# Hybrid decoder layer on one core: gate product moved ahead of the gated unit, S5 taps in 64-row tiles, another order of the last weight units, and TensorE in the last layer norm

## The chip, the cores and the metric

One Trainium2 chip, one of its cores, one launch. The metric is device time in microseconds. All data are float32; TensorE takes most operands as fp32r, split into a high and a low part.

## The reference

One decoder layer for 256 positions of width 1024:

```
proj = x @ W_in -> q, k, v, z_a (512 each), u, z_s (512 each), g_a, g_s (1024 each)
A    = (attention(q, k, v, bias) * silu(z_a)) @ W_attn_proj       8 heads x 64, causal
y    = Re(C h) + D u,  h_t = Abar h_(t-1) + Bbar u_t              32 groups x 16 channels x 64 states
B    = (GLU(gelu(y) @ W_glu) * silu(z_s)) @ W_ssm_proj
mix  = (sigmoid(g_a) * A + sigmoid(g_s) * B) @ W_out
ple  = sigmoid(x @ W_ple_gate) * (p @ W_ple_proj)
out  = LayerNorm(alpha * x + mix + ple) * g + b
```

The bias is a table of 32 buckets by 8 heads, looked up by the distance of two positions.

## The kernel before

**Weights in units.** Every large weight is cut into units of 256 rows by 512 columns (512 KB), 70 of them, in the list `units`: 40 of `w_in`, 4 of `w_ap`, 4 of `w_glu`, 8 of `w_pg`, 2 of `w_pp`, 4 of `w_sp` (units 58 to 61) and 8 of `w_out` (62 to 69). `load_next` issues the DMA of the next unit from SP's queue into one of five `raw` buffers (line 117). `split_next` makes the parts: ScalarE copies `raw` to `whi`, rounded (line 144), VectorE subtracts to get `wlo` (line 145). `whi` and `wlo` have three buffers each, so the split of a unit waits until TensorE is done with the unit three before. A unit is then 24 matmuls of 256 columns (`t_chunk`) or 12 of 512 (`n_chunk`): high by high, high by low, low by high, all from line 149. The last four units don't use `whi` and `wlo` but tiles that are free by then (`tail_w`): high parts in the buffers `xh` and `xl`, which held the split input and are read last by the `w_pg` matmuls, low parts in `tb` and `sc` of the attention.

**Order.** TensorE's order is written out by hand: it runs the matmuls in the order of the code. For the other engines a planner orders the instructions ahead of the run; what stands in `tc.high_priority()` goes first. The loop over `steps` (one step per unit up to `w_sp`) puts the next load, the evacuation of the chunk just finished and the split of unit i + 2 at high priority, then the unit's matmuls, then what `order` lists for that step. `AT` gives the steps of the work in between: `bt` the transposes of the S5 input matrix (`s5_btT`, line 383, copied out of PSUM by ScalarE on line 385), `x` the S5 inputs (`s5_xm`, `s5_x`, then the scan and `s5_h`), `sc` the attention scores and the softmax that follows one step later (`a_scores`, `a_exp`, exponentials on line 587, scaling on line 592), `kb` and `cb` the S5 kernels, `tr` and `out` the attention's transposes and products, `y` the S5 outputs. The small products use four PSUM banks (`aux`), the chunks four others (`acc`).

**S5 output.** Four positions make a step of the scan. Within such a step the input acts through taps: `s5_kbd` spreads the 16 x 16 blocks of each tap over 128 x 128 block-diagonal matrices (`Kbd`), and `s5_yt(t)` runs four matmuls with them on `uT`, of 256, 192, 128 and 64 columns. `s5_y(t)` adds the part of the carried state: 32 matmuls of 128 rows by 32 columns, into four strips of 32 output partitions. A float32 matmul (not fp32r) shows as two matmul instructions in the trace. `s5_bounce` brings the input through DRAM into `U`, where a partition holds a channel and a lag.

**End.** After step 61, `w_out`: units 62 to 65 hold its first 512 rows and 66 to 69 the rest. Each serves row tile 0 and row tile 1 (128 positions each, parameter `s` of `wo_mm`). The operands are the merged branches, `mh0`, `ml0` for the first 512 rows and `mh1`, `ml1` for the rest, written by `ev_ys` (lines 801 to 806) after units 59 and 61. `ln_in` adds the product to `xb` and takes statistics; `ln_out` normalises, on VectorE in pieces and on ScalarE and POOL for the rest, and stores. `ev_pp` (lines 788, 790) adds the per-layer term to `xb` after units 56 and 57.

Of the kernel before, what the change touches and what calls it, by code (L numbers as in the profile page):

```python
# [18 lines left out]
P = 128  # L19
# [3 lines left out]
H = 8  # L23
# [9 lines left out]
AT = dict(bt=24, x=27, sc=23, kb=27, cb=29, tr=31, out=32, y=35)  # L33
# [12 lines left out]
C_ID, C_MK, C_J, C_OH = 0, P, P + 8, P + 8 + NPH  # L46
C_W = C_OH + 257
# [10 lines left out]
def hybrid_layer_kernel(ctx: ExitStack, tc, xT, x, pT, w_in, w_ap, w_sp, w_out, par, bp, cp,  # L58
# [33 lines left out]
    mask = cs[:, C_MK:C_MK + 8]  # L92
    jmul = cs[:, C_J:C_J + NPH]
    onehot = cs[0:32, C_OH:C_OH + 257]
# [13 lines left out]

    def load_next(pieces=1):
        i = st["load"]  # L110
        if i >= len(units):
            return
        st["load"] += 1
# [8 lines left out]
    def split_next(pieces=1):  # L122
        i = st["split"]
        if i >= len(units):
            return
        st["split"] += 1
# [5 lines left out]
        else:  # L132
            if j == 0:
# [69 lines left out]
    def par_loads():  # L203
        nc.sync.dma_start(cs, cst)
        nc.sync.dma_start(br, bp)
        nc.sync.dma_start(cr, cp)
    dk = T([P, 4], "dk")
    rb = T([32, 8], "rb")
# [212 lines left out]
    def s5_kbd():  # L421
        p_ = st5["kp"]
        kb = st5["Kbd"] = T([P, 4, 4, P], "Kbd")
        V.tensor_tensor(out=kb.rearrange("p t u (g c) -> p (t u) g c", c=16),
                        in0=bc(p_[:, 0:256].rearrange("p (tu c) -> p tu c", c=16), 2, 8),
                        in1=bc(bc(mask, 1, 16), 3, 16), op=ALU.mult)
        for t in range(4):
            V.scalar_tensor_tensor(kb[:, t, 0, :], ident, dk[:, t:t + 1], kb[:, t, 0, :],
                                   op0=ALU.mult, op1=ALU.add)
# [86 lines left out]
    def s5_yt(t):  # L516
        p_ = st5[f"yp{t}"] = aux()
        kb = st5["Kbd"]
        for tau in range(4):
            n = (4 - tau) * NJ  # L520
            mm(p_[:, tau * NJ:4 * NJ], kb[:, t, tau, :],
               uT[:, t, 0:4 - tau, :].rearrange("p l j -> p (l j)"), tau == 0, False)

    def s5_y(t):
# [7 lines left out]
        if t == 0:  # L532
            st5["y"] = T([P, 4, S], "U")
# [14 lines left out]
    def a_bias():  # L548
        p_ = aux()
        nc.sync.dma_start(rb, relb)  # L550
        mm(p_[0:8, 0:257], rb, onehot, True, True)
        r8 = T([8, 384], "pt", bufs=2)
        V.memset(r8[:, 0:127], NEG)
        A.activation(r8[:, 127:384], p_[0:8, 0:257], AF.Copy)
        rs = dr.tile([8, 384], F32, name="scr_r")
        nc.sync.dma_start(rs, r8)
        nc.sync.dma_start(tb, bass.AP(tensor=rs.tensor, offset=rs.offset,
                                        ap=[[1, P], [384, H], [1, 256]]))
# [196 lines left out]
    def ev_glu(n):  # L755
# [19 lines left out]
        return f  # L775
    for n in range(2):
        t_chunk(4, lambda: (yh[0], yl[0]), ev_glu(n))

    n_chunk(8, xop, ev_tanh(new("tg0", "CAb0", (P, 2, 512))))
# [45 lines left out]


    order = {}

# [28 lines left out]
    at(AT["kb"] + 1, lambda: s5_kbm(1), s5_kbd)  # L857
# [4 lines left out]
    for t in range(4):  # L862
        at(AT["y"] + 2 * t, lambda t=t: s5_yt(t))
        at(AT["y"] + 1 + 2 * t, lambda t=t: s5_y(t))
    at(44, load_x)

    pend = None
    for i, (f, ev) in enumerate(steps):
        with tc.high_priority():
# [4 lines left out]
            split_next(2 if i < 2 else 1)  # L874
# [137 lines left out]
```

## Time and profile before

| | us |
|---|---|
| median of 3 runs | 242.12 (242.01 to 242.9) |
| the profiled execution | 242.09 |
| its span | 240.3 |
| TensorE busy | 230.3 |
| VectorE busy | 188.2 |
| ScalarE busy | 140.2 |
| POOL busy | 15.9 |
| loaded and stored through DRAM | 42.47 MB read, 1.59 MB written |

Engines: PE is TensorE's matmuls, PEld its weight loads (beside the matmuls), DVE VectorE, ACT ScalarE, POOL GpSimd, SP the queue that issues DMAs. A busy share is an average over stages with different limits, and a busy TensorE is not one at its peak, since matmuls overlap: what a stage costs is read from the times at which its instructions start. A row of the trace in order of time has the start, the time that the merged instructions took, engine, line, operation, output and inputs, shape and count, and in brackets the idle time of the engine just before, with what ended it. All times count from the start of the span.

### The profile page before, as it was taken

The numbers are of one execution on the slowest core, as the hardware profiler recorded it, in microseconds if no ns is written. First come the engines' busy times: TensorE is split into PE (matmuls) and PEld (weight loads), VectorE is DVE, ScalarE is ACT, GpSimd is POOL, SyncE is SP. The second block draws the span as 40 slices with busy tenths as digits, with TensorE's granted clock in tenths as the row PEclk, the third lists the DMA queues.
The fourth block names the chain that finished last, engine by engine and source line by source line (L and its number), as shares of the span: only waits on it lengthen the run. The fifth ranks groups of instructions, "written<-read, shape, count | busy, mean of one in ns | idle before, by whom it ended". The sixth has DMA issues, their size and how long they took to land.

```text
span 240.3 us, 5066 instructions
## 1 busy us (share of the span) xinstructions
PE 230.3 (96%) x2042; PEld 212.6 (88%) x2042; DVE 188.2 (78%) x333; ACT 140.2 (58%) x222; POOL 15.9 (7%) x17
## 2 busy tenths in 40 slices
PE   8899999999999999999999999999999999999970
PEld 6899999999978899998998999999888889988760
DVE  2879999999899986878999744485674479997395
ACT  4847554845588389999734955335565353775021
POOL 4000000000000005000000000072000000000031
PEclk9999999999999999999999999999999999999998
DMA  5999998977634484323743663664555655660013
GB/s 162 331 343 357 354 238 242 353 232 215 196 93 118 147 255 119 110 92 97 232 150 136 207 213 110 197 245 162 189 174 191 199 202 170 186 190 0 3 44 131
DMA packets 26374, 44.37 MB, mean 185 GB/s; under 512 B 4200, under 2 KB 7280, under 8 KB 26352
## 3 DMA queue, kind: packets, MB, share of 16 engines
q1 hardware_dynamic: 26064, 43.75, 57.5%
q8 instruction: 16, 0.26, 0.4%
q10 hardware_dynamic: 288, 0.31, 0.4%
q14 instruction: 6, 0.05, 0.1%
HBM read 42.47 MB, written 1.59 MB: 183 GB/s over the span
## 4 chain that ended last, share of the span: by engine, by line
PE 77%; ACT 10%; DMA 5%; DVE 4%; SPq 2%; issue 1%; ACTq 0%
PE acc L149 68%; PE aux L149 8%; DMA raw<-in_w_in 5%; ACT whi L144 4%; ACT sc L587 2%; ACT sc L592 2%; ACT CAb L436 1%; DVE wlo L145 1%; SPq L191 1%; SPq L189 1%; DVE xb L930 1%; DVE xb L920 1%; DVE st L910 1%; DVE xb L908 1%; PE aux L598 0%
## 5 line engine op out<-in xcount | busy, mean ns | idle before, releaser
L144 ACT ACTIVATE whi<-raw 128x1024 fp32r<-128x1024 f32 (+2 forms) x71 | 70.7, 997 | 59.9 <-PE acc L149 52.9
L145 DVE TENSOR_TENSOR wlo<-raw,whi 128x1024 fp32r<-128x1024 f32 (+2 forms) x71 | 81.9, 1154 | 30.3 <-ACT whi L144 29.9
L149 PE MATMUL acc<-xh,whi 128*128 128x256 f32 x288 | 47.7, 287 | 0.8 <-ACT whi L144 0.8
L149 PE MATMUL acc<-xl,whi 128*128 128x256 f32 x288 | 45.8, 281 | 0.0
L149 PE MATMUL acc<-xh,wlo 128*128 128x256 f32 x288 | 45.6, 280 | 0.0
L149 PEld LDWEIGHTS acc<-xh,whi 128*128 128x128 f32 x288 | 39.3, 190 | 2.3 <-ACT whi L144 1.3
L149 PEld LDWEIGHTS acc<-xl,whi 128*128 128x128 f32 x288 | 39.3, 189 | 0.0
L149 PEld LDWEIGHTS acc<-xh,wlo 128*128 128x128 f32 x288 | 38.9, 188 | 0.3 <-DVE wlo L145 0.3
L149 PE MATMUL acc<-whi,xh 128*128 128x512 f32 x48 | 19.0, 395 | 0.0
L149 PE MATMUL acc<-wlo,xh 128*128 128x512 f32 x48 | 19.0, 395 | 0.0
L149 PE MATMUL acc<-whi,xl 128*128 128x512 f32 x48 | 19.0, 395 | 0.0
L149 PEld LDWEIGHTS acc<-wlo,xh 128*128 128x128 f32 x48 | 9.0, 188 | 2.2
L149 PEld LDWEIGHTS acc<-whi,xh 128*128 128x128 f32 x48 | 9.0, 188 | 2.1
L149 PEld LDWEIGHTS acc<-whi,xl 128*128 128x128 f32 x48 | 9.0, 188 | 2.1
L149 PE MATMUL acc<-whi,BT 128*128 128x512 f32 (+1 forms) x32 | 9.1, 366 | 0.0
L818 POOL TENSOR_SCALAR xb<-xb 128x1024 f32<-128x1024 f32 x2 | 5.5, 2774 | 42.2 <-DMA xb<-in_x 42.2
L916 ACT ACTIVATE rs<-mv,eps 128x1 f32<-128x1 f32 x2 | 0.6, 294 | 12.1 <-DVE mv L915 12.1
L587 ACT ACTIVATE sc<-sc,nmx 128x128 f32<-128x128 f32 (+1 forms) x16 | 7.0, 442 | 0.0
L149 PEld LDWEIGHTS acc<-whi,BT 128*128 128x128 f32 x32 | 5.7, 188 | 1.1
L193 DVE TENSOR_TENSOR xl<-sc,xh 128x256 fp32r<-128x256 f32 x8 | 3.4, 420 | 4.1 <-ACT xh L192 4.1
L908 DVE TENSOR_TENSOR xb<-acc,xb 128x512 f32<-128x512 f32 (+1 forms) x4 | 2.5, 619 | 5.0 <-PE acc L149 5.0
L928 POOL TENSOR_TENSOR xb<-xb,lng 128x512 f32<-128x512 f32 (+1 forms) x2 | 1.7, 839 | 69.8 <-ACT xb L927 69.8
(254 smaller groups left out, 407.8 us busy)
## 6 DMA issues: line engine op xcount, KB each, us to landing
raw<-in_w_in SPq DMA_DIRECT2D x36, 512.0 KB, 4.7
raw<-in_w_pg SPq DMA_DIRECT2D x8, 512.0 KB, 4.6
raw<-in_w_out SPq DMA_DIRECT2D x8, 512.0 KB, 4.5
raw<-in_w_ap SPq DMA_DIRECT2D x4, 512.0 KB, 5.0
raw<-in_w_glu SPq DMA_DIRECT2D x4, 512.0 KB, 3.9
raw<-in_w_sp SPq DMA_DIRECT2D x4, 512.0 KB, 4.1
raw<-in_w_in SPq DMA_DIRECT2D x7, 256.0 KB, 4.3
sc<-in_xT SPq DMA_DIRECT2D x8, 128.0 KB, 4.0
```

The source lines that it names most:

```text
L144: A.activation(h[:, k, c], r[:, k, c], AF.Copy)
L145: V.tensor_sub(l[:, k, c], r[:, k, c], h[:, k, c].bitcast(F32))
L149: return PE.matmul(o, a, b, start=start, stop=stop, skip_group_check=True)
L189: nc.sync.dma_start(xs[:, kk], xT[:, kk])
L191: nc.sync.dma_start(t[:, k, cc], units[c][:, k, cc])
L193: V.tensor_sub(xl[:, kk], xs[:, kk], xh[:, kk].bitcast(F32))
L436: A.activation(o[rw, :, :, 16 * g2:16 * g2 + 16], st5[f"CA{part}"][rw, :, 1:5, :], AF.Copy)
L587: A.activation(sc[:, h, qs[q]], sc[:, h, qs[q]], AF.Exp, bias=nmx[:, h, q:q + 1], accum_out=sm_[:, h, q:q + 1])
L592: A.activation(sc[:, h, qs[q]], sc[:, h, qs[q]], AF.Copy, scale=sm_[:, h, q:q + 1])
L818: G.tensor_scalar(late["xb"][:, s, :], late["xb"][:, s, :], ALPHA, None, op0=ALU.mult)
L908: V.tensor_tensor(out=xb[:, s, sl], in0=(yo2 if c0 else yo[s][n])[:, 0:c1 - c0], in1=xb[:, s, sl], op=ALU.add)
L910: V.bn_stats(out=stat[s][:, c // 256, :], in_=xb[:, s, c:c + 256])
```

## The change

- **Bias.** The table of biases by distance is made on the host (`_bias`) in the layout of `tb`, and `a_bias` is one load. The one-hot constants, their matmul and the trip through DRAM go; `cst` shrinks from 462 to 213 columns.
- **Taps.** `s5_kbd` gives way to `s5_kt`: the taps go, by four strided ScalarE copies, into a compact tile `kt`, through DRAM (`kscr`, one store on SP's queue, eight loads on POOL's) into `tt`, where a partition holds a lag and a channel as in `U`. `s5_yt(t0)` does blocks `t0` and `t0 + 2` at once: 64 matmuls of 64 rows (contraction) by 32 columns, on `U` in place of `uT`. It is called twice.
- **Steps.** `bt` 24 to 27, `x` 27 to 29, `tr` 31 to 33, `out` 32 to 34, `y` 35 to 38 (with `s5_yt` in two of the steps, `s5_y` in four), `load_x` 44 to 47, `s5_abar` 1 to 3, `s5_bt` 2 to 3. The load of `br` moves from step 0 to 3, that of `cr` to 5. Units 2 and 3 are split whole, not in halves.
- **Gate ahead of the gated unit.** The first half of `w_pg` (with its `tanh`) goes before `w_glu`.
- **Last units.** `SEQ` reorders the loads and splits of the last ten units, so that 66 to 69 are loaded and split among 60 to 65; `DOUBLE` makes steps 57 to 60 load and split two units each. The square root's table is fetched in step 57 by a small activation.
- **Row tile 0 first.** Of `w_out`, unit 62 still serves both row tiles; 63, 64 and 65 serve row tile 0 only, then 66 to 69 for row tile 0; row tile 1 follows with 63, 66, 67, then all of the second 512 columns in two halves of 256.
- **Last norm.** Row tile 0's norm is wholly on VectorE. For row tile 1, columns 0 to 320 are built in PSUM by TensorE (x g - mean g + sd b, with two diagonal matrices, 320 columns in float32) and scaled by ScalarE; VectorE does the other 704 in two halves of 352. POOL has no part any more.

The diff, cut to its core:

```diff
-AT = dict(bt=24, x=27, sc=23, kb=27, cb=29, tr=31, out=32, y=35)
+AT = dict(bt=27, x=29, sc=23, kb=27, cb=29, tr=33, out=34, y=38)
+
+DOUBLE = (57, 58, 59, 60)
+SEQ = (6, 7, 0, 8, 1, 9, 2, 3, 4, 5)
...
+    def seq(j):
+
+        n = len(units)
+        return j if j < n - 10 else list(range(n - 10, n))[SEQ[j - (n - 10)]]
...
+    add_units(w_pg, D, 0, 512)
     for n in range(2):
         add_units(w_glu, 512, 512 * n, 512)
-    for n in range(2):
-        add_units(w_pg, D, 512 * n, 512)
+    add_units(w_pg, D, 512, 512)
...
-    def s5_kbd():
...
+    def s5_kt():
+
+        p_ = st5["kp"][:, 0:256].rearrange("p (t u c) -> p t u c", t=4, u=4)
+        kt = T([P, 4, 4, 16, 4], "kT", nm="kt")
+        G.memset(kt, 0.0)
+        for l in range(L):
+            A.activation(kt[:, :, l, :, l:4].rearrange("p t c u -> p t u c"), p_[:, :, 0:4 - l, :],
+                         AF.Copy)
+        m16 = bc(cs[:, C_M16:C_M16 + 16], 1, 4)
         for t in range(4):
+            d = kt[:, t, 0, :, 0]
+            d = bass.AP(tensor=d.tensor, offset=d.offset, ap=[list(d.ap[0]), [65, 4], list(d.ap[1])])
+            V.scalar_tensor_tensor(d, m16, dk[:, t:t + 1], d, op0=ALU.mult, op1=ALU.add)
+        nc.sync.dma_start(kscr.rearrange("(t q) l d -> q t (l d)", q=P),
+                          kt.rearrange("q t l c u -> q t (l c u)"))
+        tt = st5["tt"] = T([P, 16, 2, 64], "Kbd", nm="tt")
+        G.memset(tt[:, :, 1, :], 0.0)
+        v = kscr.rearrange("(r m c) l d -> r l c m d", r=2, c=16)
+        for r in range(2):
+            for l in range(L):
+                b0 = 64 * r + 16 * (L - 1 - l)
+                nc.gpsimd.dma_start(tt[b0:b0 + 16, :, 0, :], v[r, l])
...
-    def s5_yt(t):
-        p_ = st5[f"yp{t}"] = aux()
-        kb = st5["Kbd"]
-        for tau in range(4):
-            n = (4 - tau) * NJ
-            mm(p_[:, tau * NJ:4 * NJ], kb[:, t, tau, :],
-               uT[:, t, 0:4 - tau, :].rearrange("p l j -> p (l j)"), tau == 0, False)
+    def s5_yt(t0):
+        for t in (t0, t0 + 2):
+            st5[f"yp{t}"] = aux()
+        tt = st5["tt"].rearrange("p m z d -> p (m z d)")
+        for l in range(L):
+            for g2 in range(2):
+                for gpt in range(4):
+                    for r in range(2):
+                        t = t0 + 2 * r
+                        gpp = 4 * (t % 2) + gpt
+                        rw = slice(64 * r, 64 * r + 64)
+                        o = 128 * (2 * gpp + g2) - 64 * g2 + l
+                        mm(st5[f"yp{t}"][32 * gpt:32 * gpt + 32, l * NJ:(l + 1) * NJ],
+                           tt[rw, o:o + 125:4], U[rw, gpp, g2, :], l == 0 and g2 == 0, False)
...
-        if t == 0:
-            st5["y"] = T([P, 4, S], "U")
+        if "y" not in st5:
+            st5["y"] = T([P, 4, S], "uT", nm="y")
...
     def a_bias():
-        p_ = aux()
...
-        nc.sync.dma_start(tb, bass.AP(tensor=rs.tensor, offset=rs.offset,
-                                        ap=[[1, P], [384, H], [1, 256]]))
+        nc.sync.dma_start(tb, relb)
...
-    at(0, par_loads)
+    at(0, lambda: nc.sync.dma_start(cs, cst))
     at(0, *[hp_(f) for f in (s5_scalars, s5_angles, s5_phases)])
-    at(1, hp_(s5_abar))
-    at(2, lambda: s5_bt(0), lambda: s5_bt(1))
+    at(3, lambda: nc.sync.dma_start(br, bp), hp_(s5_abar), lambda: s5_bt(0), lambda: s5_bt(1))
-    at(5, lambda: s5_ca(0), lambda: s5_ca(1))
+    at(5, lambda: nc.sync.dma_start(cr, cp), lambda: s5_ca(0), lambda: s5_ca(1))
...
-    at(AT["kb"] + 1, lambda: s5_kbm(1), s5_kbd)
+    at(AT["kb"] + 1, lambda: s5_kbm(1), s5_kt)
...
-    for t in range(4):
-        at(AT["y"] + 2 * t, lambda t=t: s5_yt(t))
-        at(AT["y"] + 1 + 2 * t, lambda t=t: s5_y(t))
-    at(44, load_x)
+    for t in range(2):
+        at(AT["y"] + 4 * t, lambda t=t: s5_yt(t))
+        at(AT["y"] + 1 + 4 * t, lambda t=t: s5_y(t))
+        at(AT["y"] + 3 + 4 * t, lambda t=t: s5_y(t + 2))
+    at(47, load_x)
+    at(57, sqrt_table)
...
-            split_next(2 if i < 2 else 1)
+            split_next()
+            if i in DOUBLE:
+                load_next()
+                split_next()
...
-    def ln_out(s, dve, pool_):
...
+    def ln_stats(s):
+        keep(V.bn_aggr(out=mv[s], in_=stat[s]))
+        keep(A.activation(rs[s], mv[s][:, 1:2], AF.Sqrt, bias=late["eps"]))
+    def sub(s, c0, c1):
+        sl = slice(c0, c1)
+        keep(V.scalar_tensor_tensor(xb[:, s, sl], xb[:, s, sl], mv[s][:, 0:1], g[:, sl],
+                                    op0=ALU.subtract, op1=ALU.mult))
+
+    def scale(s, c0, c1):
+        sl = slice(c0, c1)
+        keep(V.scalar_tensor_tensor(xb[:, s, sl], xb[:, s, sl], nm[s], b[:, sl],
+                                    op0=ALU.mult, op1=ALU.add))
+        nc.sync.dma_start(out[P * s:P * s + P, sl], xb[:, s, sl])
+
+    def ln_out0():
+        ln_stats(0)
+        sub(0, 0, 512)
+        keep(V.reciprocal(nm[0], rs[0]))
+        scale(0, 0, 512)
+        sub(0, 512, 1024)
+        scale(0, 512, 1024)
+    dg = [T([P, P], f"dg{i}") for i in range(2)]
+    xg = T([P, FW], "xg")
+    hp = aux()
+
+    def ln_pre():
+        keep(V.tensor_mul(xg, xb[:, 1, 0:FW], g[:, 0:FW]))
+
+    def ln_out1():
+        mm(hp[:, 0:FW], ident, xg, True, False)
+        ln_stats(1)
+        keep(V.tensor_scalar(dg[0], ident, mv[1][:, 0:1], -1.0, op0=ALU.mult, op1=ALU.mult))
+        mm(hp[:, 0:FW], dg[0], g[:, 0:FW], False, False)
+        keep(A.activation(dg[1], ident, AF.Copy, scale=rs[1]))
+        mm(hp[:, 0:FW], dg[1], b[:, 0:FW], False, True)
+        h = (FW + D) // 2
+        sub(1, FW, h)
+        keep(V.reciprocal(nm[1], rs[1]))
+        scale(1, FW, h)
+        keep(A.activation(xg, hp[:, 0:FW], AF.Copy, scale=nm[1]))
+        nc.scalar.dma_start(out[P:2 * P, 0:FW], xg)
+        sub(1, h, D)
+        scale(1, h, D)
...
     u = nmain
+    for i, (n, kk) in enumerate(((0, 0), (0, 2), (1, 0), (1, 2))):
+        load_next()
+        split_next()
+        wo_mm(u + i, kk, n, 0)
+        if i == 0:
+            wo_mm(u, kk, n, 1)
     for n in range(2):
-        for kk in (0, 2):
-            load_next()
-            split_next()
-            wo_mm(u, kk, n, 0)
-            if n:
-                wo_mm(u, kk, n, 1, 0, 256)
-                wo_mm(u, kk, n, 1, 256, 512)
-            else:
-                wo_mm(u, kk, n, 1)
-            u += 1
-    load_next()
-    split_next()
-    split_next()
-    for n in range(2):
-        wo_seq([(u + 2 * n, 4), (u + 2 * n + 1, 6)], n, 0)
+        wo_seq([(u + 4 + 2 * n, 4), (u + 5 + 2 * n, 6)], n, 0)
         ln_in(0, n)
-    wo_seq([(u, 4), (u + 1, 6)], 0, 1)
-    ln_out(0, [(0, 512)], (512, 1024))
+    wo_seq([(u + 1, 2), (u + 4, 4), (u + 5, 6)], 0, 1)
+    ln_out0()
     ln_in(1, 0)
+    ln_pre()
     for c in (0, 256):
-        wo_seq([(u + 2, 4), (u + 3, 6)], 1, 1, c, c + 256)
+        wo_seq([(u + 2, 0), (u + 3, 2), (u + 6, 4), (u + 7, 6)], 1, 1, c, c + 256)
         ln_in(1, 1, c, c + 256)
-    ln_out(1, [(0, 544), (544, 928)], (928, 1024))
+    ln_out1()
```

## Rows read from the trace of the kernel before

**Rows 1.** Page, first part: busy time, share of the span and instructions.
```profile
PE 230.3 (96%) x2042; PEld 212.6 (88%) x2042; DVE 188.2 (78%) x333; ACT 140.2 (58%) x222; POOL 15.9 (7%) x17
```

**Rows 2.** Windows: stretch, length, each engine's busy time (instructions), granted clock, DMA.
```profile
87.00:112.40 25.40, 25.40 (x372) 24.34 (x370) 18.71 (x43) 24.60 (x63) 3.56 (x2) 1.00 0.38 112
194.40:221.00 26.60, 26.60 (x173) 24.04 (x172) 26.03 (x32) 15.48 (x17) 0.00 (x0) 1.00 0.49 156
```

**Rows 3.** Chain of waits: start, length, piece; where it leaves TensorE.
```profile
230.12 0.69 DVE xb L908
```

**Rows 4.** Timeline, TensorE, the bias matmul and the unit behind it.
```profile
32.11 0.59 PE L149 MATMUL aux<-cst,rb 32*8 32x257 f32 x2
32.63 0.74 PE L149 MATMUL acc<-xh,whi 128*128 128x256 f32 x4
```

**Rows 5.** Timeline, TensorE, one `s5_yt` and one `s5_y` of four each.
```profile
143.44 1.31 PE L149 MATMUL aux<-uT,Kbd 128*128 128x256 f32 x8
144.56 0.72 PE L149 MATMUL acc<-qT,whi 128*128 128x256 f32 x4
...
147.58 1.10 PE L149 MATMUL aux<-BT,CAb 128*32 128x64 f32 x64
148.61 0.75 PE L149 MATMUL acc<-qT,whi 128*128 128x256 f32 x4
```

**Rows 6.** Groups by form: count, busy us, mean ns of one, idle before.
```profile
L149 PE MATMUL aux<-BT,CAb 128*32 128x64 f32 x256 | 4.4, 221 | 0.0
```

**Rows 7.** Timeline, ScalarE and TensorE, units 2 and 4.
```profile
11.18 0.63 ACT L144 ACTIVATE whi<-raw 128x512 fp32r<-128x512 f32 x1
...
11.73 0.63 PE L149 MATMUL acc<-xh,whi 128*128 128x256 f32 x4
...
17.46 0.74 PE L149 MATMUL acc<-xh,whi 128*128 128x256 f32 x4
...
18.72 0.74 PE L149 MATMUL acc<-xh,wlo 128*128 128x256 f32 x4
```

**Rows 8.** Groups by line, ScalarE, 87.0 to 112.4 us.
```profile
L587 ACT ACTIVATE sc<-sc,nmx 128x128 f32<-128x128 f32 (+1 forms) x16 | 7.0, 442 | 0.0
L144 ACT ACTIVATE whi<-raw 128x1024 fp32r<-128x1024 f32 x6 | 6.2, 1047 | 0.0
L592 ACT ACTIVATE sc<-sc,sms 128x128 f32<-128x128 f32 (+1 forms) x16 | 6.0, 441 | 0.0
```

**Rows 9.** Timeline, VectorE, first and last of 194.4 to 221.0 us.
```profile
194.40 1.23 DVE L145 TENSOR_TENSOR wlo<-raw,whi 128x1024 fp32r<-128x1024 f32 x1 [1.59 <-ACT whi L144]
...
217.43 2.35 DVE L145 TENSOR_TENSOR sc<-raw,xl 128x1024 fp32r<-128x1024 f32 x2
219.70 1.28 DVE L806 SCALAR_TENSOR_TENSOR kT<-A,qT 128x512 fp32r<-128x512 f32 x2
```

**Rows 10.** Timeline, TensorE, the S5 transposes and what follows them.
```profile
78.78 1.03 PE L383 MATMUL aux<-cst,A 128*128 128x128 f32 x8
80.28 0.33 PE L149 MATMUL aux<-ks,qs 128*128 128x128 f32 x1 [0.47 <-ACT BT L385]
...
85.49 0.33 PE L149 MATMUL aux<-ks,qs 128*128 128x128 f32 x1 [0.29 <-ACT BT L385]
...
112.77 1.24 PE L149 MATMUL aux<-pt,vN 128*64 128x256 f32 x8 [0.23 <-ACT pt L602]
```

**Rows 11.** Timeline, TensorE, after the gate, unit 66 and the last matmul.
```profile
193.32 0.39 PE L149 MATMUL acc<-whi,ph 128*128 128x512 f32 x1
...
221.51 0.39 PE L149 MATMUL acc<-xh,qT 128*128 128x512 f32 x1
...
232.67 0.27 PE L149 MATMUL aux<-sc,qT 128*128 128x256 f32 x1
```

**Rows 12.** Timeline, VectorE, the last norm.
```profile
234.20 0.88 DVE L920 SCALAR_TENSOR_TENSOR xb<-xb,mv,lng 128x544 f32<-128x544 f32 x1
...
236.76 0.62 DVE L930 SCALAR_TENSOR_TENSOR xb<-xb,rs,lnb 128x384 f32<-128x384 f32 x1
```

More of the change, by code (lines that the diff above doesn't have):

```diff
@@ L43 @@
 TWO_PI = float(np.nextafter(np.float32(2 * math.pi), np.float32(0)))
-C_ID, C_MK, C_J, C_OH = 0, P, P + 8, P + 8 + NPH
-C_W = C_OH + 257
+C_J, C_M16, C_ID = 0, NPH, NPH + 16
+C_W = C_ID + P
 def bc(ap, axis, n):
@@ L107, in hybrid_layer_kernel @@
     st = dict(load=0, split=0)
+    def seq(j):
+        n = len(units)
+        return j if j < n - 10 else list(range(n - 10, n))[SEQ[j - (n - 10)]]
     def load_next(pieces=1):
-        i = st["load"]
-        if i >= len(units):
+        if st["load"] >= len(units):
             return
+        i = seq(st["load"])
         st["load"] += 1
@@ L122, in split_next @@
     def split_next(pieces=1):
-        i = st["split"]
-        if i >= len(units):
+        if st["split"] >= len(units):
             return
+        i = seq(st["split"])
         st["split"] += 1
@@ L132, in split_next @@
         else:
-            if j == 0:
+            if not tail_w:
                 tail_w.update(h0=T([P, 2, 2, 512], "xh", F32R), h1=T([P, 2, 2, 512], "xl", F32R),
@@ L419, in s5_kbm @@
                        part == 0, part == 1)
-    def s5_kbd():
[L422 to L426, printed above, removed]
-        for t in range(4):
-            V.scalar_tensor_tensor(kb[:, t, 0, :], ident, dk[:, t:t + 1], kb[:, t, 0, :],
-                                   op0=ALU.mult, op1=ALU.add)
+    kscr = dr.tile([512, 4, 64], F32, name="scr_k")
+    def s5_kt():
[6 more added lines that the diff above has]
+        m16 = bc(cs[:, C_M16:C_M16 + 16], 1, 4)
+        for t in range(4):
+            d = kt[:, t, 0, :, 0]
[10 more added lines that the diff above has]
+                nc.gpsimd.dma_start(tt[b0:b0 + 16, :, 0, :], v[r, l])
     def s5_cabd(part):
@@ L548, in a_bias @@
     def a_bias():
-        p_ = aux()
[L550 to L556, printed above, removed]
-        nc.sync.dma_start(tb, bass.AP(tensor=rs.tensor, offset=rs.offset,
-                                        ap=[[1, P], [384, H], [1, 256]]))
+        nc.sync.dma_start(tb, relb)
     def rev(h, last, n):
@@ L775, in ev_glu @@
         return f
+    n_chunk(8, xop, ev_tanh(new("tg0", "CAb0", (P, 2, 512))))
     for n in range(2):
         t_chunk(4, lambda: (yh[0], yl[0]), ev_glu(n))
-    n_chunk(8, xop, ev_tanh(new("tg0", "CAb0", (P, 2, 512))))
     n_chunk(8, xop, ev_tanh(new("tg1", "CAb1", (P, 2, 512))))
@@ L824, in load_x, with sqrt_table @@
         V.memset(late["eps"], EPS)
+    def sqrt_table():
+        A.activation(rs[0], late["eps"], AF.Sqrt)
     order = {}
+    rs = [T([P, 1], f"rs{s}") for s in range(2)]
     def at(i, *f):
@@ L902, in hybrid_layer_kernel @@
     mv = [T([P, 2], f"mv{s}") for s in range(2)]
-    rs = [T([P, 1], f"rs{s}") for s in range(2)]
     nm = [T([P, 1], f"nm{s}") for s in range(2)]
@@ new lines, in hybrid_layer_kernel @@
+    g, b = late["g"], late["b"]
+    keep = tc.keep_in_program_order
+    FW = 320
+    def ln_stats(s):
[10 more added lines that the diff above has]
+        nc.sync.dma_start(out[P * s:P * s + P, sl], xb[:, s, sl])
@@ L970, in _constants, with _bias @@
     c[:, C_ID:C_ID + P] = np.eye(P, dtype=np.float32)
-    c[:, C_MK:C_MK + 8] = (np.arange(P)[:, None] // 16 == np.arange(8)[None]).astype(np.float32)
     c[:, C_J:C_J + NPH] = np.concatenate([np.arange(5), L * np.arange(NJ)]).astype(np.float32)
-    for d in range(257):
-        b = d if d < 16 else min(31, 16 + int(math.log(d / 16) / math.log(8) * 16))
-        c[b, C_OH + d] = 1.0
-    return c
+    c[:, C_M16:C_ID] = (np.arange(P)[:, None] % 16 == np.arange(16)[None]).astype(np.float32)
+    return c
+def _bias(relb):
+    b = [d if d < 16 else min(31, 16 + int(math.log(d / 16) / math.log(8) * 16)) for d in range(257)]
+    r = np.concatenate([np.full((127, 8), NEG, np.float32), relb[b]]).T
+    return np.ascontiguousarray(np.stack([r[:, p:p + 256] for p in range(P)]))
 def _layout(i):
```

29 lines of the change are left out of this document (1 added, 28 removed).

## The prediction

> **What bounds the kernel now.** I read the page first: TensorE is busy for 96% of the span [rows 1]. Busy time alone proves little, since matmuls overlap, so next I read TensorE's instructions in order of time. They stand edge to edge: four 256-column matmuls every 0.47 us, one unit of weights (24 of them) every 2.83 us, with gaps of a few tenths only. The granted clock is 1.00 of full speed, the 2.4 GHz level, in every stretch that I looked at [rows 2]. So up to the last matmul the time is a list of TensorE pieces, and an edit on another engine counts only where it makes TensorE wait. After that the chain of waits passes to VectorE, which does the last layer norm [rows 3]. The third reading is the one that decides here: in 194.4 to 221.0 VectorE is busy for 26.03 of 26.60 us [rows 2]. It is a second bound there, hidden just behind TensorE.
>
> The sum is made against the profiled execution, 242.09 us (span 240.3, 1.8 outside it); the median of the three runs is 242.12. Half a per cent (1.2 us) is about what a measurement of this kernel can tell from no change.
>
> **Bias table.** The matmul with the one-hot constants leaves TensorE's list (its table comes ready from the host, same 1 MB load): 32.11 to 32.63 [rows 4], with the change of shape in front of it **-0.55**. Nothing waits for it early; one answer.
>
> **Taps.** A `s5_yt` before holds TensorE for 1.12 us (143.44 to 144.56), four of them 4.48 [rows 5]. The new one does two blocks in one call: 64 products of 64 rows by 32 columns, two matmul instructions each, so 128 instructions, and two calls. The nearest row is `s5_y`: 64 instructions of the same 64-column width on four column strips. The group lasts 1.10 and one instruction 0.22, so they start within 0.88 us, 14 ns apiece [rows 5, 6]; with the change of shape in front they hold TensorE for about 1.12, 0.24 over the 0.88. The new form has twice as many separate pieces of the array (two row halves by four strips), so 14 ns becomes 7 ns if all eight run side by side: 128 x 7 = 0.9, plus 0.24, twice is 2.3. If only four do: 128 x 14 = 1.8, plus 0.24, twice is 4.1. Ends: -2.2 and -0.4. I take **-2.1**, because the strips of [rows 5] already overlap fully and row halves are a further split of the same kind.
>
> The 14 ns also speak against a rule. The Trainium skill, page "TensorE: Matmul & The Clock Gate", section "Wait — 56ns, not 53.3ns?", says that start to start never falls below about 25 ns however narrow the matmul is. By that the two calls would take 2 x (128 x 25 + 240 ns) = 6.9 us, 2.4 more than now; the trace does not agree with the rule for column strips.
>
> What feeds the taps moves to other engines: four strided ScalarE copies from PSUM in place of VectorE's wide multiply, a store on SP's queue, eight loads on POOL's queue. Between the block sums (step 28) and the first use (step 38) lie ten steps of 2.83 us or more, which cover the round trip through DRAM. Queued behind the store on SP are the weight loads, five buffers deep; queued behind the loads on POOL is the small memset that the scan needs. With the cover gone each would cost what they are late; I take nothing, up to 1 us.
>
> **Start.** Units 2 and 3 are split whole, no longer in halves. ScalarE took the second half of unit 2 at 11.18, and TensorE began that unit at 11.73 [rows 7]. A whole split takes ScalarE 1.05 [rows 8]: ready at 12.2, 0.5 late; the low part follows after VectorE's 1.23 [rows 9], another 0.3 late. Against that the wait inside unit 4 goes (17.46 to 18.72 holds 0.94 of work, so 0.3) [rows 7]. **+0.4**, ends -0.2 and +0.9. Moving `br` and `cr` behind more weight loads is free: no wait of TensorE after 20 us is put down to a load.
>
> **Middle.** The transposes of `s5_btT` now cost two waits: 78.78 plus eight at 0.11 is 79.65, and the next matmul starts at 80.28, because ScalarE must empty a bank: 0.63. The second, ahead of 85.49, is 0.29 by its mark and about 0.45 by the same count. With 0.23 to 0.4 before 112.77 [rows 10] that is 1.5 us of waits. The change puts the transposes three steps later, followed by `s5_kbm`, which needs one bank, not two, and the attention's transposes two steps later. The bound below is -1.5. Above: the copies of the transposes now land amid the exponentials, where ScalarE is busy 24.6 of 25.4 us [rows 2]; see the second rival, +5.4. I take **-0.8**: part of the wait goes.
>
> **Gate ahead of the gated unit.** `w_pg`'s first half before `w_glu`: the same matmuls, and more time between the last `s5_y` and its reader. The `tanh` of the gate then needs `CAb0` free, which step 45 sees to. Nothing.
>
> **The last units, split early.** VectorE's 26 us in 194.4 to 221.0 are 12 low-part splits (two in 2.35, so 1.14 to 1.2 each) and 20 instructions of about 0.62 to 0.64 (two in 1.28) [rows 9]. The last ends at 220.98, and TensorE needs it at 221.51 [rows 9, 11]: half a microsecond of slack. The change doesn't remove any of it. It cannot start earlier either: the early units go into `xh` and `xl`, which the gate's matmuls read until 193.3 [rows 11], and the split at 194.40 is the first thing then ready. But it is wanted sooner, since row tile 0 is finished first: three units of row tile 1 (1.40 each: eight units took 210.3 to 232.8, so 2.81 for two tiles) move behind it, so TensorE reaches the units of the second half 4.2 us earlier, at 217.3.
> - Work is conserved: VectorE ends at 194.4 + 26.1 = 220.5 at the earliest. If the last thing is the second half of `ml1`, TensorE has 1.2 (rest of that unit) + 2.8 + 4.2 + 5.7 = 13.9 left, and ends at 234.4, not 232.8: +1.6. If it is the low part of unit 65, 16.4 are left: +4.1.
> - The written order says the same from the front: before the low part of unit 62 stand nine splits and 14 short ones, 9 x 1.14 + 14 x 0.62 = 19.0, done at 213.4, while TensorE wants it at 210.8, 2.6 late.
>
> In the trace before, the `ml1` writes did come last [rows 9], so I stay near the low end: **+2.0**, ends 0 (the planner finds room before 194.4, where VectorE idled for 1.59) and +4.1. The table load for the square root, now in step 57, lies on ScalarE, which has room there.
>
> **Last norm.** Before, from the last matmul (232.67 + 0.12) to the last VectorE instruction (236.76 + 0.62) are 4.6 us [rows 11, 12]. After, row tile 0's norm is done under the matmuls of row tile 1. Then: the same sum and statistics up to 234.20 (1.4), the diagonal (an estimate of 0.2 from the 128-wide work around it), and four instructions of 352 columns at about 0.53 (384 columns took 0.62 [rows 12]) with a reciprocal, 2.25 together: 3.85. **-0.7**, ends -1.2 and 0. The other 320 columns go by TensorE and ScalarE at the same time. The last store is as long as before.
>
> **Sum.** -0.55 - 2.1 + 0.4 - 0.8 + 2.0 - 0.7 = -1.75: **240.3 us**.
>
> **Rivals.**
> - *VectorE doesn't bind at the end* (0 in place of +2.0): 238.3. For it: only 1.6 of the price is forced, and that by an order of VectorE's list. Against: 26.03 busy of 26.60.
> - *The copies of the transposes come late; slower.* Place: ScalarE, 87 to 100 us. By order of writing, the exponentials and scalings of three of four head pairs stand ahead: three quarters of 7.0 + 6.0 is 9.8 [rows 8], plus three splits of 1.05, from about 87.2 to 100.1. TensorE comes to the second transposes at about 78.8 + 3 x 0.92 + 4 x 2.83 + 1.5 = 94.3, and needs a bank that the first copy frees. It decides from the point where ScalarE reaches that copy after 94.3. Price: up to 5.4 plus the 0.8 not saved, up to 246.5, 243.7 if half of it comes about. Against: the planner can slip a copy into any gap where a reciprocal is awaited.
> - *The change does not speed the taps* (four pieces side by side): 1.7 back, 242.0.
> - *The row halves get in each other's way*: every start waits for the other half, 28 ns, twice the 14 of [rows 5, 6]. Two calls are then 2 x (128 x 28 + 240 ns) = 7.6 us, 3.2 more than now: 242.09 - 1.75 + 2.1 + 3.2 = 245.6. Against it: the strips show nothing of the kind. (By the skill's rule above, 2.4 more: 244.8.)
>
> **How the numbers follow.** Forecast 0.42 (239.3 to 241.5 for itself); VectorE not binding 0.17; taps as before 0.14; late copies 0.24; the halves in each other's way 0.03. Of the forecast about 0.33 lies beyond half a per cent (under 240.9) and 0.09 within; the first rival is all faster; the third within; late copies slower but for 0.02. Faster 0.50, same 0.25, slower 0.25. The range goes from 237.3 (VectorE not binding, and the wait in the middle wholly gone) to 244.5 (late copies at a little over half of their price).
>
> **What would show it.** Right: two groups of 128 narrow matmuls about 1.1 us long; no wait near 94 us; a wait of TensorE for VectorE's low parts of some 2 us between 207 and 217; VectorE without a gap from the last gate matmul until the last `ml1` write; under 4 us between the last matmul and the last VectorE instruction. Wrong: tap groups near 2 us, TensorE waiting for the copies of `BT` near 94 us, or no wait at all before `w_out`'s units. The likeliest error is the order of VectorE's list, which I cannot see.

## The result: slower, and where the time went

The changed kernel takes 258.94 us (median of four runs), the kernel before 242.32 (with a fourth run) on the same chip: a ratio of 1.065, with an interval of 1.0575 to 1.0732. Its slowest run (260.84) lies in a slower state and is left out of the ratio, as is the slowest of the kernel with both edits below; without it the median is 258.2, and every gain over the changed kernel that is given below as a difference of medians is 0.7 us smaller. The profiled execution took 256.8 us (span 254.9), 14.6 more of span than before; it is the fastest of the four. The page first: its busy times, then the granted clock in 40 slices (each 6.4 us).

```profile
PE 233.1 (91%) x2270; PEld 212.2 (83%) x2270; DVE 185.8 (73%) x331; ACT 148.2 (58%) x230; POOL 19.0 (7%) x23
...
PEclk9999999999999999679999999999999999769999
```

Against [rows 1] TensorE has hardly more work but a lower share, so it waits. VectorE has less work, ScalarE 8 us more. And the granted clock, 1.00 in the stretches read before, falls in two places. TensorE's timeline shows waits in the same two places:

```profile
95.49 0.60 PE L384 MATMUL aux<-cst,A 128*128 128x128 f32 x4
97.53 0.66 PE L384 MATMUL aux<-cst,A 128*128 128x128 f32 x4 [1.44 <-ACT BT L386]
...
101.72 0.33 PE L155 MATMUL aux<-U,BT 64*64 64x64 f32 x4
107.61 1.12 PE L155 MATMUL aux<-U,BT 64*64 64x64 f32 x28 [5.56 <-ACT BT L386]
...
217.00 0.63 PE L155 MATMUL acc<-sh,wlo 128*128 128x256 f32 x4
220.53 0.80 PE L155 MATMUL acc<-whi,BT 128*128 128x512 f32 x1 [2.90 <-ACT BT L819]
224.01 0.79 PE L155 MATMUL acc<-whi,BT 128*128 128x512 f32 x1 [2.68 <-DVE BT L820]
```

In the middle TensorE waits 7.0 us (1.44 and 5.56) for ScalarE's copies of the S5 transposes (`BT`), at the end 5.6 us (2.90 and 2.68) for the merged branches `mh0`, `ml0` (which lie in the buffers `BT0`, `BT1`). From within the wait of 5.56 us, and again behind that of 2.90, there is a stretch at a lower clock. The windows (length, busy time of PE, PEld, DVE, ACT, POOL, clock, DMA):

```profile
104.60:111.40 6.80, 3.79 (x41) 3.67 (x42) 1.95 (x5) 6.80 (x20) 0.00 (x0) 0.52 0.47 151
220.70:227.50 6.80, 4.12 (x10) 2.89 (x11) 5.66 (x9) 1.89 (x3) 0.00 (x0) 0.52 0.00 0
```

0.52 is the 1.2 GHz level. What it costs is read from pieces at either level: the unit behind the wait, 108.66 to the next group at 112.80, took 4.14 in place of 3.02 (the same stretch before, 98.65 to 101.67), and the 28 products before it about 0.5 more: 1.6 us. At the end eight 512-column matmuls from 224.01 to 227.43 took 3.4 us in place of 1.9: 1.6 again.

The account, in the profiled executions: the first matmul of the scores starts at 75.03 before and 75.00 after, so all that comes earlier cancels (partly by a faster pace of the matmuls in this one execution, see the last section). From there: a new wait for a low part at 77.80, +0.8; the middle +7.0 and +1.6, less 1.5 of the old waits in [rows 10]; taps -1.4; the end, from the time at which the first matmul of `w_out` was possible (217.47, when TensorE was through with step 61) to its last one (247.47), 30.0 in place of 22.4, +7.6; the last norm -0.6. That is 13.5 of the 14.2 us by which the last VectorE instruction is later; the rest I did not place.

### The profile page after: what moved, and what is told of

It reads as the page before. It is cut to its first block, busy times and chain, and to the rows that moved or that the text cites. A ratio compares the mean times of both kernels' runs of the same rounds, so it can differ in the third digit from the quotient of the medians.

```text
span 254.9 us, 5563 instructions
## 1 busy us (share of the span) xinstructions
PE 233.1 (91%) x2270; PEld 212.2 (83%) x2270; DVE 185.8 (73%) x331; ACT 148.2 (58%) x230; POOL 19.0 (7%) x23
## 4 chain that ended last, share of the span: by engine, by line
PE 55%; DVE 20%; ACT 11%; issue 6%; DMA 5%; SPq 1%; DVEq 0%; ACTq 0%
PE acc L155 47%; PE aux L155 6%; DVE wlo L151 6%; ACT whi L150 3%; ACT sc L602 3%; DMA sc<-in_xT 2%; DMA raw<-in_w_in 2%; DMA Ct<-in_pT 1%; ACT sc L607 1%; DVE qs L718 1%; DVE xb L804 1%; DVE sc L151 1%; DVE B L374 1%; DVE A L373 1%; DVE kl L729 1%
## 5 line engine op out<-in xcount | busy, mean ns | idle before, releaser
L151 DVE TENSOR_TENSOR wlo<-raw,whi 128x1024 fp32r<-128x1024 f32 (+2 forms) x69 | 80.9, 1175 | 39.9 <-ACT whi L150 39.2
L150 ACT ACTIVATE whi<-raw 128x1024 fp32r<-128x1024 f32 (+2 forms) x69 | 70.0, 1020 | 60.7 <-PE acc L155 48.9
L155 PE MATMUL acc<-whi,BT 128*128 128x512 f32 (+1 forms) x32 | 10.8, 419 | 5.6 <-ACT BT L819 2.9
L155 PEld LDWEIGHTS acc<-whi,BT 128*128 128x128 f32 x32 | 6.6, 213 | 7.6 <-DVE BT L820 3.2
L449 POOL MEMSET CAb<- 128x2048 f32 x2 | 3.6, 1806 | 84.1 <-PE aux L155 84.1
L155 PE MATMUL aux<-U,BT 64*64 64x64 f32 x128 | 3.5, 245 | 5.6 <-ACT BT L386 5.6
L155 PEld LDWEIGHTS aux<-U,BT 64*64 64x64 f32 x128 | 2.8, 152 | 6.2 <-ACT BT L386 5.7
```

The lines of the kernel that those rows point to most:

```text
L150: A.activation(h[:, k, c], r[:, k, c], AF.Copy)
L151: V.tensor_sub(l[:, k, c], r[:, k, c], h[:, k, c].bitcast(F32))
L155: return PE.matmul(o, a, b, start=start, stop=stop, skip_group_check=True)
L449: G.memset(o, 0.0)
```

## Experiments

Theory A: the middle is the place of the `BT` copies in ScalarE's list. Theory B: the end is VectorE's work on the early splits, ahead of what `w_out` needs first. Theory C came from the trace: the small square root brings table loads. Where nothing else is said, the ratio is to the kernel before, beside it on the chip.

**The copies by VectorE** (step 27 kept).

```diff
-            A.activation(dst[...], p_, AF.Copy)
+            V.tensor_copy(dst[...], p_)
```

> The changed kernel with one edit: the four copies of the S5 transposes out of PSUM go by VectorE in place of ScalarE, at the same steps (bt=27). Theory A (TensorE stands still near 97 and 102 to 107.6 us because these copies stand behind exponentials, splits and scalings in ScalarE's list): both waits go (1.44 + 5.56 us), and the granted clock does not fall behind them (the unit at 108.7 took 4.1 us in place of 2.83, the 28 products ahead of it 1.05 in place of 0.6): about 8.7 us less than the changed kernel, 248 to 251 us. Rival (ScalarE is late with its whole list, and the weight splits on it are what TensorE meets next): at least half of the wait comes back as a wait for whi, 254 us or more.

Measured: 252.18 us, 1.042 [1.038, 1.046]. The copies now run at 94.31 and 99.34, and TensorE's waits there are gone; two smaller ones are left:

```profile
93.35 0.65 PE L155 MATMUL aux<-C,Bbd 128*32 128x64 f32 x32 [1.07 <-DVE wlo L151]
109.95 0.68 PE L155 MATMUL aux<-U,BT 64*64 64x64 f32 x28 [0.89 <-ACT kt L430]
```

7.0 us of waits became 2.0, and the clock holds there. The gain is 6.8 of medians, not 8.7, and the time lies just outside my range: those 2.0 us are left. Theory A holds for the place; the end is as it was.

**The same copies on ScalarE, at high priority.** In its list this moves only the second pair.

```diff
-            A.activation(dst[...], p_, AF.Copy)
+            with tc.high_priority():
+                A.activation(dst[...], p_, AF.Copy)
```

> The changed kernel with the four copies of the S5 transposes still on ScalarE, but at high priority for the planner. In ScalarE's list the first pair keeps its place (behind eight exponentials, two copies for CAb and a split), the second pair moves ahead of seven exponentials, the two copies to Bbd and a split, some 5 us of work. Theory A (it is the place in ScalarE's list that TensorE waits for) gives a part of the whole: the wait of 1.44 near 97 stays, that of 5.56 near 102 falls to about 1, and the granted clock does not fall behind it (1.7 us): 4.5 to 6.5 us less than the changed kernel, 252.5 to 254.5. Rival (ScalarE's total amount of work there): the wait returns ahead of a weight split, 256 or more.

Measured: 253.21 us, 1.047 [1.045, 1.050], within the range.

```profile
97.42 0.66 PE L384 MATMUL aux<-cst,A 128*128 128x128 f32 x4 [1.46 <-ACT BT L387]
102.97 0.68 PE L155 MATMUL aux<-U,BT 64*64 64x64 f32 x28 [1.02 <-ACT BT L387]
```

The first wait stayed (1.44, now 1.46), the second fell from 5.56 to 1.02: only the wait whose copy was moved became shorter. The engine and the work are the same, only the place in the list is another.

**The transposes back in steps 24 and 25.**

```diff
-AT = dict(bt=27, x=29, ...
+AT = dict(bt=24, x=29, ...
```

> The changed kernel with the S5 transposes back in steps 24 and 25 (x stays at 29, all else as changed). Theory A (late copies on ScalarE): the copies stand ahead of the exponentials again, the two waits of 7.0 us and the low clock behind them go, and the two short waits of the kernel before (0.64 and 0.45) come back: 7.6 us less than the changed kernel, 249.5 to 252. Rival (the later scan and the new copies of the taps make ScalarE late, whatever the step of the transposes): the wait ahead of the first S5 input stays, 255 or more.

Measured: 253.18 us, 1.046 [1.042, 1.050]: 5.8 less, not 7.6, and outside my range. The two waits go, the old short ones are back, and TensorE now waits for a weight split on ScalarE:

```profile
110.63 0.74 PE L155 MATMUL acc<-xh,whi 128*128 128x256 f32 x4 [1.00 <-ACT whi L150]
```

So something like the rival is true too: ScalarE has little to spare there. And the end is longer here, 31.4 us in place of 30.0: behind the same waits the low clock lasted for 10 us, not 7.

**The last ten units in natural order**, one split per step; row tile 0 still first.

```diff
-DOUBLE = (57, 58, 59, 60)
-SEQ = (6, 7, 0, 8, 1, 9, 2, 3, 4, 5)
+DOUBLE = ()
+SEQ = (0, 1, 2, 3, 4, 5, 6, 7, 8, 9)
...
+    load_next()
+    split_next()
+    split_next()
     for n in range(2):
         wo_seq([(u + 4 + 2 * n, 4), (u + 5 + 2 * n, 6)], n, 0)
```

> The changed kernel with the last ten units loaded and split in their natural order, one per step (the last two before row tile 0 is finished), but still used in the new order: row tile 0 first, TensorE in the last norm. Theory B (the early splits stand in VectorE's list ahead of the merged branches that all of w_out needs first): the waits of 3.1 and 3.3 us at 217 and 221 go, and the low clock behind them (about 3 us): 9 us less than the changed kernel, 248 to 251. Rival (VectorE simply has too much to do there, so row tile 0 first must wait in any order): 254 or more, with the wait moved to the units of the second half.

Measured: 255.9 us, 1.058 [1.052, 1.063]: only 3 less, a miss. The waits for `mh0` and `ml0` are gone as theory B said, but two others stand in their place, and behind them the clock fell here too (to 0.50, from 231 to 234):

```profile
227.82 0.50 PE L155 MATMUL acc<-wlo,BT 128*128 128x512 f32 x1 [1.35 <-DVE wlo L151]
...
230.69 0.53 PE L155 MATMUL acc<-xh,kT 128*128 128x512 f32 x1 [1.45 <-DVE kT L820]
```

The end, counted as above from the time at which `w_out` is possible (here 220.38) to its last matmul, is 27.0 us in place of 30.0. The rival had said 254 or more and a wait moved to the second half: its number held, and so did the second of these waits.

**Both: transposes in 24 and 25, natural order.**

> Both edits at once: transposes in steps 24 and 25, last ten units in natural order. If A and B are two separate places, the gains add up: 16 to 17 us less than the changed kernel, 240 to 243 us, about the kernel before. If one of them only uncovers the other, 246 or more.

Measured: 248.61 us, 1.025 [1.018, 1.032]; its four executions lie between 246.6 and 251.05, with a mean clock of 0.982 to 0.999. That is some 10 us less, not 16: by its number it falls to the case that one place only uncovers the other, but the two gains measured singly (5.8 and 3.0) do add up, and it was their sizes that I had too large. The end in the profiled execution (246.6, the fastest), where the clock held behind nearly the same two waits:

```profile
219.14 0.50 PE L155 MATMUL acc<-wlo,BT 128*128 128x512 f32 x1 [1.21 <-DVE wlo L151]
...
222.01 0.51 PE L155 MATMUL acc<-xh,kT 128*128 128x512 f32 x1 [1.45 <-DVE kT L820]
```

I read these 2.66 us as what row tile 0 first costs by itself (the forecast's +2.0); the next run tries it. VectorE has the same work here as with the early splits, only in another order, and the stage from the end of step 61 to the last matmul of `w_out` is 25.3 us in place of 31.4: it is the place of the early splits that costs.

**And the order of use of the kernel before**, units 62 to 65 for both row tiles first. The code of `w_out` is that of the kernel before, with the new norm.

> Transposes back in steps 24 and 25, the last ten units in natural order, and in addition the order of use of the kernel before: units 62 to 65 serve both row tiles before 66. TensorE stays in the last norm. Beside the kernel with the natural order alone (246.6 in its profiled run, 248.6 median), row tile 0 first has cost two waits there, 1.21 for a low part and 1.45 for ml1: without it both go, 2.5 to 3 us less, 243.5 to 246. Rival (VectorE ends at the same time, so the wait returns at unit 66): less than 1 us.

Measured: 246.29 us, 1.018 [1.014, 1.022], just outside the range: 2.3 of medians, 1.1 of the profiled executions. No wait of TensorE is left in `w_out`, and its stage falls from 25.3 to 22.2 us, as before the change. But from there to the end of the span it is 1.4 us longer in this order, with the new norm, and that takes part of the gain back. So of the end's 7.6 us some 2.7 to 3.1 belong to the order of row tiles, and the rest, with the low clock behind it, to the early splits.

**The merged branches kept ahead of the later splits** (transposes in 24 and 25, early splits kept).

```diff
+                tc.keep_in_program_order(...)   # on each instruction of ev_ys, VectorE and ScalarE
...
+            if st["split"] > 65:
+                tc.keep_in_program_order(d)     # on the splits from there on
```

> The kernel with the transposes back in steps 24 and 25, and one edit more: the merged branches (the first half ahead of the splits of the units from the sixth of the last ten on) are kept in the order of the code on VectorE and ScalarE; the four early splits stay early. Theory B (order in VectorE's list, not its amount): mh0 and ml0 are ready near 217, the waits of 3.1 and 3.2 us and the low clock behind them go, and about 2.6 us come back as a wait for the last thing in VectorE's list: 246 to 248.5 us. Rival (amount of work, or the loads of the raw weights, which ScalarE waits for there): 251 or more.

Measured: 254.08 us, 1.050 [1.044, 1.057], no gain over 253.18. By its number the rival held, but the trace shows that the edit did more than I meant:

```profile
211.50 0.63 ACT L824 ACTIVATE BT<-Bbd 128x512 fp32r<-128x512 f32 x1 [4.97 <-DVE Bbd L821]
...
216.78 1.22 PE L159 MATMUL acc<-whi,BT 128*128 128x512 f32 x2 [3.62 <-ACT whi L150]
```

By order alone `ml0` came earlier: it is complete at 215.56, 2.6 us after `w_out` could have begun; in the changed kernel at 225.15, 7.7 after. But the order of the code held on ScalarE too. There the splits of units 69 and 62 now stand behind the copies for `mh0`, which wait 4.97 and 2.08 us for VectorE, and so the split of unit 62 is late instead. This run therefore does not separate order from amount; the natural order above does, which takes 6 us less with the same work on VectorE. Nor are the loads of the weights what binds there: in the changed kernel VectorE has no gap from 201.68 to 226.36.

**Without the small square root.**

```diff
-    at(57, sqrt_table)
```

> The changed kernel without the small square root that was to fetch its table in step 57. The trace shows its table load at 2.01 us, right behind the first table, and six more loads of 1.28 us between 23 and 46 us and at 89: the planner put the square root at the start, since nothing holds it back. Theory C (these loads delay the splits and the S5 preparation, and so cause the waits of TensorE for low parts at 65.7, 71.7 and 76.8 us, 1.85 together): ScalarE's busy time falls by about 8 us, the three waits go, 1.5 to 2.5 us less than the changed kernel, 255 to 257. Rival (the waits come from the later S5 preparation in step 3): the busy time falls but the waits stay, 257 to 260. Under either the waits near 97, 102 and 217 us stay, since the order of ScalarE's list is the same there.

Measured: 257.12 us, 1.062 [1.058, 1.065], just outside the range. In the changed kernel ScalarE's table loads were these, and one more ahead of the exponentials as before:

```profile
0.72 1.28 ACT L185 ACT_TABLE_LOAD   x1 [0.72 <-PEq L1050]
2.01 1.28 ACT L841 ACT_TABLE_LOAD   x1
23.59 1.28 ACT L317 ACT_TABLE_LOAD   x1
30.88 1.28 ACT L694 ACT_TABLE_LOAD   x1
39.04 1.28 ACT L315 ACT_TABLE_LOAD   x1
42.43 1.28 ACT L699 ACT_TABLE_LOAD   x1
44.83 1.28 ACT L316 ACT_TABLE_LOAD   x1
```

Without it only the first remains of these, ScalarE's busy time is 140.3, and TensorE does not wait between 60 and 80 us (in the changed kernel it does at 72.57 and 77.80). Theory C holds for those waits. Their price is not shown: 1.8 us of medians lies within the spread of the changed kernel's runs, and the profiled execution is no faster (257.16 against 256.8), since its matmuls up to 65 us ran at the slower of the two paces of the last section.

**What had cost time put back** (the steps `bt`, `x`, `tr` and `out`, the start, the last units and the row tiles as before, no square root; the bias, taps, gate and norm of the change stay, and so do its steps `y` and `load_x`).

> What is left when all that cost time is put back: the table of biases from the host, the taps in 64-row tiles, the gate ahead of the gated unit and TensorE in the last norm stay; steps (bt 24, x 27, tr 31, out 32), start, order of the last units and of the row tiles are those of the kernel before, and the small square root is gone. If these parts have the prices that the traces show (bias -0.5, taps 4.58 to 3.13, so -1.4, last norm -0.6) and nothing else is lost: 242.1 - 2.5 = 239.6, 238.8 to 240.5. If the copies of the taps on ScalarE make a split late near 108 us: 241 to 242.5.

Measured: 244.74 us, 1.010 [1.007, 1.013]: 1% over the kernel before, and 5 us over what I expected. The trace names three things. A split is late near 108 us; TensorE stands still for 1.49 inside an `s5_y`, where the profile shows nothing that it waits for; and the norm is longer, not shorter:

```profile
109.50 0.74 PE L155 MATMUL acc<-xh,whi 128*128 128x256 f32 x4 [0.89 <-ACT whi L150]
...
143.31 0.88 PE L155 MATMUL aux<-BT,CAb 128*32 128x64 f32 x48 [1.49 <-issue]
...
234.58 0.81 PE L155 MATMUL aux<-xg,cst 128*128 128x320 f32 x2 [0.34 <-DVE xg L966]
237.18 0.81 PE L155 MATMUL aux<-lng,dg 128*128 128x320 f32 x2 [1.80 <-DVE dg L971]
```

From the last matmul of `w_out` to the end of the span it is 8.7 us here and in the run with the old order of row tiles above, 7.5 before, 7.3 in the changed kernel. The new norm puts all of row tile 0 on VectorE, and that hides only behind the longer row tile 1 of the new order.

**Taps and bias alone, on the kernel before**: with the copies of the taps on ScalarE, then on VectorE.

```diff
-            A.activation(kt[...], p_[...], AF.Copy)
+            V.tensor_copy(kt[...], p_[...])
```

> The kernel before with two parts of the change alone: the table of biases from the host, and the taps in 64-row tiles (four copies on ScalarE, the way through DRAM, two calls at steps 35 and 39). By the prices in the traces (bias -0.5; taps 4.58 to 3.13, so -1.45) 240.0 us, 239.5 to 240.7. Rival (the copies of the taps delay a weight split on ScalarE near 108 us, as seen in the kernel with most parts undone, 1.05 there): 241 to 242, no measurable change.

> The same with the four strided copies of the taps on VectorE in place of ScalarE. VectorE loses its wide multiply (2.28) there and has gaps of 0.8 and 1.8 us near 106 and 109. If the copies on ScalarE are what makes a split late: no wait near 108, 240.0 us, 239.5 to 240.7, and faster than the one with the copies on ScalarE by up to 1 us. If the wait near 108 has another cause: both alike.

Measured: 242.29 us, 1.0015 [0.9995, 1.0036], and 241.39 us, 0.998 [0.996, 1.000]. Neither differs from the kernel before by half a per cent. The profiled executions (240.9 and 239.84) are each the fastest of twelve, so their times are not the rule; they show the gains on TensorE, but the wait near 108 us is in both, first with the copies on ScalarE, then on VectorE:

```profile
109.50 0.74 PE L147 MATMUL acc<-xh,whi 128*128 128x256 f32 x4 [0.65 <-ACT whi L142]
...
108.20 0.74 PE L147 MATMUL acc<-xh,whi 128*128 128x256 f32 x4 [0.89 <-ACT whi L142]
...
87.00:110.00 23.00, 22.06 (x340) 20.63 (x339) 16.17 (x37) 22.28 (x54) 9.10 (x11) 1.00 0.50 138
```

(The last row, a window, is of the one with the copies on VectorE.) So it was not the copies. ScalarE is busy for 22.28 of 23.0 us there, about as it was before [rows 2, 8]: it is a second bound. In that profile TensorE stands 2.39 us ahead of the kernel before at one unit (99.91 against 102.30), most of it by the faster pace, and 1.25 two units later (108.20 against 109.45): half of the lead is lost there. With the copies on ScalarE it stands 0.85 ahead (101.45) and then level (109.50): all of it is lost.

## Why the prediction was wrong, step by step

**Bias** (-0.55): gone from TensorE's list as worked out. But I priced it through to the end; with taps and bias alone, half of TensorE's lead in one profile and all of it in the other was lost at ScalarE's full stretch near 108 us.

**Taps** (-2.1): right in sign, mis-sized. A call holds TensorE for 1.56 us, not 1.14:

```profile
144.26 1.63 PE L155 MATMUL aux<-U,tt 64*32 64x64 f32 x128
145.82 0.74 PE L155 MATMUL acc<-xh,whi 128*128 128x256 f32 x4
```

Two calls are 3.1 in place of 4.48: -1.4, between the two ends. Less 0.24 for the change of shape that is 10 ns a start, between the 7 that I took and the 14 of four strips. So the eight pieces gain on four, but not by half, and the 28 ns of the rival (each half waiting for the other) did not come. The rule of the Trainium skill ("TensorE: Matmul & The Clock Gate", section "Wait — 56ns, not 53.3ns?"), at about 25 ns from start to start, would make a call 3.2 us plus the change of shape; the trace shows less than half of that.

**Start** (+0.4): too small. Unit 2 starts at 12.33, before at 11.73 [rows 7]: 0.6, near the 0.5 worked out. But unit 3 starts at 15.99 in place of 14.56 and unit 4 at 19.18 in place of 17.46 [rows 7]: 1.7. I counted one whole split as late, and let it cancel against an old wait. That nothing of it is left at 75 us is luck: the faster pace of this one execution, which I had not forecast, is worth about as much (up to 1.7).

**Middle** (-0.8, taken at a chance; +5.4 in the rival): this is the first step that failed. The engine was named, and one point: at the second transposes TensorE wants a bank before ScalarE has reached the first copy. That wait came, 1.44 us. The greater one, 5.56, stands one step further on, at the first S5 inputs. By the code these read only what the first pair of copies wrote, done at 97.9; what releases them by the trace is the first copy of the second pair, so it can only be its bank that they need. "TensorE waiting for the copies of `BT` near 94 us" was among the prediction's signs of being wrong, but it has no term for that second wait, nor for the clock behind it (1.6). And I gave the rival 0.24 and bounded it by one reading of ScalarE's list. In the trace the first pair of copies stands behind eight exponentials, two copies for `CAb` and a split:

```profile
93.80 2.11 ACT L452 ACTIVATE CAb<-C 64x1024 f32<-64x1024 f32 x2
95.94 1.06 ACT L150 ACTIVATE whi<-raw 128x1024 fp32r<-128x1024 f32 x1
96.90 1.07 ACT L386 ACTIVATE BT<-aux 128x512 f32<-128x512 f32 x2
...
106.97 1.07 ACT L386 ACTIVATE BT<-aux 128x512 f32<-128x512 f32 x2
```

The second pair starts at 106.97; my bound for the list was 100.1. Two errors make up these 6.9 us. The exponentials start at 90.27, not at 87.2: 3.1. And I counted exponentials, scalings and splits, but not the copies to `CAb` and `Bbd` and the first pair to `BT`, which stand ahead of the second pair as well: 2.1, 1.0 and 1.0. (The splits took 0.3 less than I had counted.) "The planner can slip a copy into any gap" was the reason against; the planner did not.

**Gate ahead, kt's way through DRAM** (0): no wait of TensorE for `tt` or for the gate shows.

**Last units split early** (+2.0, 0 to +4.1): the second step that failed; +7.6. The work on VectorE was summed right. Its last write comes 25.8 us behind the end of the gate's matmuls (226.36 and 200.61), and I had 27.2. What I got wrong is which instruction matters. I asked what comes last; TensorE has other work while that is made. But the early splits also stand ahead of `mh0` and `ml0`, which `w_out` needs first, and `w_out` is all of the kernel's remaining work on TensorE but for the norm's few products:

```profile
203.51 1.22 DVE L151 TENSOR_TENSOR tb<-raw,xh 128x1024 fp32r<-128x1024 f32 x1
...
205.85 1.22 DVE L151 TENSOR_TENSOR tb<-raw,xh 128x1024 fp32r<-128x1024 f32 x1
...
209.92 1.22 DVE L151 TENSOR_TENSOR sc<-raw,xl 128x1024 fp32r<-128x1024 f32 x1
...
214.53 1.22 DVE L151 TENSOR_TENSOR sc<-raw,xl 128x1024 fp32r<-128x1024 f32 x1
215.66 1.28 DVE L815 SCALAR_TENSOR_TENSOR ts<-ts,acc 128x512 f32<-128x512 f32 x2
...
223.27 0.68 DVE L820 SCALAR_TENSOR_TENSOR BT<-Bbd,BT 128x512 fp32r<-128x512 f32 x1
```

My count from the front (nine splits, 14 short instructions, 2.6 late) looked for unit 62 only; up to the first part of `ml0`, which the second matmul of `w_out` waits for, it is 11 splits and 16 short ones, 22.3 us from 201.68 on. Of the 7.6, the order of row tiles by itself is some 2.7, close to the +2.0; the forecast had no term for the wait for `mh0` and `ml0` and the 1.6 us of low clock behind it. "ScalarE has room there" for the square root in step 57 was wrong in another way: the load was never in step 57.

**Last norm** (-0.7): -0.6 up to the last VectorE instruction (247.59 to 251.59 in place of [rows 11, 12]), but -0.2 up to the end of the span, since the last store ends 3.3 us after that instruction in place of 2.9. And it needs the new order of row tiles: with the old one the end is 1.2 longer than before the change.

The sum of the forecast was -1.75. The loss is in the main the two failed steps: with their measured sizes (+7.1 and +7.6) in it, the sum comes to +11.75 of the 14.2 us that were measured; with my upper ends for them (+5.4 and +4.1) it comes to +6.55.

## What to carry to other kernels

Where an engine off the critical path is busy for 95% of a stretch, as ScalarE here, count everything that it does there before moving a step into the stretch, and expect that a gain made ahead of it may be lost in it; give the rival that names such an engine the greater chance. One late copy out of PSUM can hold up a later user of its bank as well: follow the banks on to the next user. When work is made early on a full engine, ask what it now stands ahead of, and price the wait of the first thing needed, not of the last. An instruction that waits for nothing (here the table fetched early) can be put far from where it is written, so look for it in the list.

## What the runs showed of the hardware that I had not expected

- In the changed kernel the granted clock fell to its lower level during TensorE's wait of 5.56 us and again at 220.4, at the end of the wait of 2.90; it cost 1.6 us each time. Behind waits of 1.46 and 1.02 in the middle (the copies at high priority) it held. But the waits alone do not tell: at the end with the units in natural order it fell behind 1.35 and 1.45, and held behind 1.21 and 1.45 in the kernel with both edits. What decides between the two, these runs do not show.
- The table load of the small square root at 2.01 us brought five more of 1.28 us between 23 and 46 us, at the lines of the sines and of the gates in turn; without it none of them is there.
- At a granted clock of 1.00 four 256-column matmuls start to start took 0.45 us from 18 to 65 us in the changed kernel's profile, 0.47 in that of before:

```profile
20.54 0.62 PE L155 MATMUL acc<-xh,whi 128*128 128x256 f32 x4
20.99 0.62 PE L155 MATMUL acc<-xl,whi 128*128 128x256 f32 x4
```

The same faster pace stands in other profiles in other stretches (20 to 65 us with the taps' copies on VectorE, 145 to 155 with them on ScalarE). Over 16 units it is worth up to 1.7 us, more than several of the terms above. What sets it stays open, and so does the cause of the pause of 1.49 us in `s5_y`.
